# A streaming encoder trunk in fp32: moved weight splits, a delayed recurrence, an earlier attention and a last norm in two halves

## The chip, the cores and the metric

The kernel runs on one core of one Trainium2 chip. The core has a matrix engine (TensorE, PE in the profile; its weight loads are listed apart as PEld), three engines for elementwise work (VectorE = DVE, ScalarE = ACT, GpSimd = POOL), and SyncE (SP), which here issues nearly all transfers between memory and the core. PE writes its sums into banks of the PSUM memory, from which the other engines read. Each engine works through its own list of instructions in order; an instruction that must wait for another engine holds up everything behind it in its list. The metric is the device time of one execution, in microseconds (us).

## The reference

1056 tokens (1024 of a prompt, 32 of a sample with earlier state) pass through two layers of width 1024. Every sublayer ends in a layer norm over the sum with its input.

```python
# layer 0: mLSTM, then SwiGLU; layer 1: attention over a window, then SwiGLU
q, k, v, o, ig, fg = split(x @ w_in)
h = recurrence(q, k * DK**-0.5, v, ig, log_sigmoid(fg), C0, n0, m0)     # 8 heads, chunk by chunk
h = h * rsqrt(mean(h*h) + 1e-6) * g_norm * sigmoid(o)
x = layer_norm(alpha * x + h @ w_out_a)
x = layer_norm(alpha * x + (silu(x @ w_g) * (x @ w_u)) @ w_down)

k, v = split(x @ w_kv)                      # one set, 2 heads of 64; rows of a cache ahead of the sample's
s = (x @ w_q) @ k.T * 64**-0.5 + alibi      # 16 heads; 64-token chunks, own and two before
p = exp(s - max) / (sum(exp(s - max)) + exp(sink - max))
x = layer_norm(alpha * x + (p @ v) @ w_out_b)
x = layer_norm(alpha * x + (silu(x @ w_g) * (x @ w_u)) @ w_down)
```

The outputs are x, the last state of the recurrence, and the keys and values of the last window.

## The kernel before

**Numbers in two halves.** Each fp32 matrix is cut into a high and a low part (`hi` is the value cast to the matrix engine's input type, `lo` is the value less `hi`), and each product is three matmuls: hi·hi, hi·lo, lo·hi (`gemm`, L333 to 344; the three are L341, L342, L343). Activations lie with features across partitions: `ACT` holds the fp32 values and `SX` their parts, 8 tiles of 128 features by 1056 tokens. Tokens are taken in three groups (384, 384, 288), four quarters of 264, or nine chunks of 128 (the last of 32).

**The written order.** The order of all instructions is fixed when the program is built, by a small planner. Dense products are written one k-step (three matmuls) after another; after each step `wv.tick(us)` (class `Weave`, L63) hands the other tasks a time allowance `us` = 3·(max(columns, 256)/2400 + 0.003): 0.339 for 264 columns, 0.329 for 256, 0.489 for 384. A task is a generator that writes some instructions and then yields a pace: the allowance that must pass before it goes on. So a pace is a number of k-steps between two writes, not a time on the chip. `drain` writes the rest of a task at once, with no product between. `pipeline` (L92) runs a chain of stages over items, each stage a given lag behind the one before and with a pace after each step.

**Weights.** Class `Weights` (L119) keeps one list of all weights in order of use. A unit (128 x up to 1024) comes in by a transfer from SP's queue into one of `RAW` = 3 buffers (`wr`), and is split in two halves; or two units together give seven factors, for the FFN tiles that save one product in eight. A split is a cast on ACT (`wh`, L188) and a subtraction (`wl`, L190) on POOL, or on DVE for units listed in `on_vector`. Split halves lie in `SLOTS` = 5 slots, or in a place of their own (`home`). `factor` writes the splits up to the one asked for; `done` frees a unit's slots and writes the next splits as far as slots allow. Since the splits are written at that point, they stand in ACT's and POOL's order behind all that was written before.

**Stages, and where they lie in the span (us).**

- 0 to 93: the input is split, and the q, k, v of the first two heads (a pair) and all gates are projected.
- 93 to 345: the recurrence (`mlstm`, launched by `begin`, L794) is woven between the projections of pairs 1 to 3: three query groups, three key groups, and nine chunks of values (`proj_v`, L534). Its stages are `first`, `pre` (which fetches the rows `nm`, L671, and adds the mask on POOL, L693), `scores` (L703), `values` and `last`. A pair must be finished before the buffers of the pair after next are given out.
- 345 to 440: output gates (`proj_o`, L829), with an exponential on ACT (L836) that empties PE's bank and a chain on DVE after it. The last two feature tiles, 6 and 7, are done group by group while the buffers of the stage are handed over (L880), and after each, two early splits of the output weights are written.
- 440 to 570: output projection A (`mixer_out`, L897), 8 tiles of 8 steps for each of four quarters, with the norm (`ln_task`, L378; `norm_tail`, L442) of a quarter woven under the products of the next: two sums by PE over a 128 x 128 matrix, squares on ACT, products on DVE, at last a scale and shift for each of eight tiles on ACT (L427).
- 570 to 1005: the up projection of the FFN. The first `FIRST` = 2 blocks are plain products (`up_plain`, L1013), while `sums` (L1033) builds sums of the input on the elementwise engines; the others are tiles of seven factors (`up_tile`, L1076), whose results `stage` (L973) sums, splits and sends to memory. A tile's first product is copied out of its bank by ACT (L1094) when the tile has moved on.
- 1005 to 1250: the down projection (L1205); its last part is plain, with the norm (L1265).
- 1250 to 1296: keys and values for each of three groups, and four query tiles of the first group (`k_group`, `v_group`, `q_group`; loop at L1370). `k_part` splits keys into both halves of the partitions (L1308, L1310).
- 1296 to 1484: attention, 72 items (eight pairs of heads by nine chunks). An item's scores (L1424, L1425) go through DVE (a sum and minimum, L1430), ACT (exponential), DVE and POOL (division), PE (transposition), ACT and DVE (split), PE (values) and DVE (`place`). Scores, transposition and values each yield the pace `GAP_A`. The other query projections stand between. Before this, `v_turn` (L1393) turns the values to token-major, and no item's values may be written until all nine chunks are turned.
- 1484 to 1660: output projection B and its norm; 1660 to 2338: the second FFN, the same as the first; 2338 to 2359: the rest of the last norm, after the last product.

In projection B, the weights of the first quarter are read a second time for the other three. Six of eight units of that second reading have places of their own; the first reading uses the five slots. Each tile asks for its halves just before its product (`wcols`, `W.get`).

## Time and profile before

| | before |
| --- | --- |
| median of 3 runs | 2355.39 us (2355.15 to 2357.9) |
| the profiled execution: run / span | 2360.31 / 2358.5 us |
| mean granted TensorE clock | 0.982 |
| PE busy | 2240.9 us, 95% of the span |
| DVE / ACT / POOL busy | 1433.7 / 1025.8 / 1139.2 us |
| moved | 289.72 MB, 123 GB/s |

The profile is of one execution. Its page has the busy time of each engine, the span in 40 slices, the chain of work that ended last, and groups of instructions by line. From the trace come three further views that are used below. *Stretches*: the busy time and number of instructions of each engine between two points of the span, with the granted clock of TensorE, the DMA share and GB/s. *Groups by line and shape*: number, busy time, mean ns of one, then the idle time of the engine directly before them and what ended it. *Timeline*: single instructions as "start, duration, engine, line, operation, output<-inputs, shape"; in square brackets the idle time before it and the instruction that ended that. Times are us from the start of the span. A matmul's duration reaches from its start to its modelled end; the starts of two that follow each other show the rate.

### The profile page before, as it was taken

Reading aid. Unit: us, or ns where it says so; the run is one execution under the profiler, and the core shown is the slowest. Engines: PE = TensorE matmul, PEld = TensorE weight load, DVE = VectorE, ACT = ScalarE, POOL = GpSimd, SP = SyncE. Lnnn points to the kernel's source line nnn. Section 1 sums busy time; section 2 is a strip of 40 time slices with the busy share of each in tenths; the row PEclk is TensorE's granted clock in tenths of the full one; section 3 lists DMA queues with packets and bytes.
Section 4 is the critical chain, followed back from the end, with each engine's and each line's share of the span. In section 5 each row is a group of like instructions: output and inputs, shape, how many; then the busy total and the mean of one; then the engine's idle time right before and its main releaser. Section 6 shows DMA issues by size and latency. Waiting matters only on the chain. (4 is left out here: it accounts for less than half of the span.)

```text
span 2358.5 us, 44346 instructions
## 1 busy us (share of the span) xinstructions
PE 2240.9 (95%) x17218; PEld 2180.1 (92%) x17218; DVE 1433.7 (61%) x2724; ACT 1025.8 (43%) x2306; POOL 1139.2 (48%) x1054
## 2 busy tenths in 40 slices
PE   8899989899999999999999899889999999999997
PEld 8788879899999999999999789789999999999996
DVE  4344456558655555476667678767765555556655
ACT  3343345346444344322246677736434444432124
POOL 1434332326655556554313676724756665654420
PEclk9999999899999999999999999999999999999998
DMA  3111211301333334597423210331244333398712
GB/s 141 61 48 57 54 39 54 135 19 55 146 139 136 146 137 155 182 317 254 162 80 110 70 43 21 102 116 37 82 155 155 146 146 124 131 318 270 243 50 74
DMA packets 165091, 289.72 MB, mean 123 GB/s; under 512 B 15824, under 2 KB 120840, under 8 KB 164880
## 3 DMA queue, kind: packets, MB, share of 16 engines
q1 hardware_dynamic: 160528, 282.56, 35.2%
q10 hardware_dynamic: 4352, 4.33, 0.5%
q8 instruction: 135, 2.21, 0.4%
q14 instruction: 76, 0.62, 0.1%
HBM read 203.89 MB, written 82.94 MB: 122 GB/s over the span
## 5 line engine op out<-in xcount | busy, mean ns | idle before, releaser
L190 POOL TENSOR_TENSOR wl_s<-wr,wh_s 128x512 fp32r<-128x512 f32 x224 | 316.5, 1432 | 316.1 <-ACT wh_s L188 251.5
L341 PE MATMUL d<-sx,wh 128*128 128x264 f32 (+2 forms) x1152 | 374.7, 325 | 19.6 <-ACT sx L371 9.8
L343 PE MATMUL d<-sx,wl 128*128 128x264 f32 (+2 forms) x1152 | 358.7, 311 | 5.1 <-POOL wl L190 5.1
L342 PE MATMUL d<-sx,wh 128*128 128x264 f32 (+2 forms) x1152 | 358.0, 311 | 1.5 <-DVE sx L372 1.5
L188 ACT CAST wh_s<-wr 128x512 fp32r<-128x512 f32 x224 | 136.0, 618 | 328.5 <-DVE wr L167 300.5
L190 POOL TENSOR_TENSOR wl<-wr,wh 128x512 fp32r<-128x512 f32 (+2 forms) x130 | 175.7, 1374 | 208.1 <-ACT wh L188 191.8
L341 PE MATMUL A<-sx,wh_s 128*128 128x264 f32 x896 | 254.6, 284 | 0.0
L342 PE MATMUL A<-sx,wh_s 128*128 128x264 f32 x896 | 254.2, 284 | 0.0
L343 PE MATMUL A<-sx,wl_s 128*128 128x264 f32 x896 | 254.1, 284 | 0.0
L341 PEld LDWEIGHTS d<-sx,wh 128*128 128x128 f32 x1152 | 222.7, 193 | 27.4 <-ACT wh L188 10.8
L343 PEld LDWEIGHTS d<-sx,wl 128*128 128x128 f32 x1152 | 222.1, 193 | 7.5 <-POOL wl L190 7.5
L342 PEld LDWEIGHTS d<-sx,wh 128*128 128x128 f32 x1152 | 223.0, 194 | 2.9 <-DVE sx L372 2.3
L341 PE MATMUL d<-sx,ex 128*128 128x264 f32 x624 | 184.0, 295 | 12.8 <-ACT z L836 6.5
L343 PE MATMUL d<-sx,ex 128*128 128x264 f32 x624 | 181.1, 290 | 6.7 <-DVE ex L190 5.0
L342 PE MATMUL d<-sx,ex 128*128 128x264 f32 x624 | 180.0, 289 | 0.0
L190 POOL TENSOR_TENSOR wl_a<-wr,wh_a 128x512 fp32r<-128x512 f32 x112 | 153.5, 1372 | 41.3 <-ACT wh_a L188 41.3
L343 PEld LDWEIGHTS A<-sx,wl_s 128*128 128x128 f32 x896 | 168.8, 188 | 0.0
L341 PEld LDWEIGHTS A<-sx,wh_s 128*128 128x128 f32 x896 | 168.5, 188 | 0.1
L342 PEld LDWEIGHTS A<-sx,wh_s 128*128 128x128 f32 x896 | 168.4, 188 | 0.0
L1448 POOL TENSOR_SCALAR s<-s,st 128x256 f32<-128x256 f32 (+1 forms) x144 | 122.5, 864 | 58.2 <-DVE st L1446 32.9
L341 PE MATMUL A<-ex,wh_s 128*128 128x264 f32 x448 | 129.1, 288 | 10.9 <-ACT z L1094 10.9
L984 POOL TENSOR_TENSOR z<-z 128x528 fp32r<-128x528 f32 x76 | 111.9, 1472 | 51.4 <-ACT z L983 45.4
(272 smaller groups left out, 7179.8 us busy)
## 6 DMA issues: line engine op xcount, KB each, us to landing
wr<-in_gu SPq DMA_DIRECT2D x96, 512.0 KB, 4.4
hs_x<-z SPq DMA_DIRECT2D x72, 528.0 KB, 3.7
hs_t<-z SPq DMA_DIRECT2D x64, 528.0 KB, 2.9
sx<-hs_x SPq DMA_DIRECT2D x112, 264.0 KB, 5.3
sx<-hs_t SPq DMA_DIRECT2D x64, 264.0 KB, 6.0
ex<-hs_t SPq DMA_DIRECT2D x64, 264.0 KB, 6.0
wr<-in_dn SPq DMA_DIRECT2D x32, 512.0 KB, 6.3
ex<-hs_x SPq DMA_DIRECT2D x32, 264.0 KB, 5.3
```

What stands on the lines that cost most here:

```text
L188: self.nc.scalar.copy(hi, r)
L190: eng.tensor_sub(lo, r, hi.bitcast(F32))
L341: nc.tensor.matmul(out, ah, bh, start=start and k == 0, stop=False, **kw)
L342: nc.tensor.matmul(out, ah, bl, start=False, stop=False, **kw)
L343: nc.tensor.matmul(out, al, bh, start=False, stop=stop and k == last, **kw)
L984: eng.tensor_sub(lo.bitcast(F32R), buf(s), hi)
L1448: nc.gpsimd.tensor_scalar_mul(p[:R, h, lo:256], p[:R, h, lo:256], st[:R, 2, h : h + 1])
```

## The change

1. **Recurrence.** A task `go` with a pace of 5.0 is launched after the recurrence; `pre` may begin only when it has ended. The stage `first` is not held back.
2. **Query weights.** After the second and the fifth chunk of values of pairs 1 to 3 (`c` = 2 and 5), one half of the next unit (query weights of the next pair; after the last, the first output-gate unit) is split, into places of their own. `_next` returns without a split when the place is still held by a unit in use.
3. **Last output gates.** For tiles 6 and 7, `W.done` comes after the two early splits instead of between product and exponential.
4. **Up weights.** The second halves of the plain up units are subtracted on DVE instead of POOL, in both layers (2 blocks x 2 halves of the tokens x 2 units); `sums` yields 2.6 instead of 2.2; `stage` yields 2.0 before its first split.
5. **Attention.** Only the first group's keys, values and queries are made ahead; then all parts of the norm before it and the cached keys and values are written, and the attention is launched. Keys and values of groups 1 and 2 follow, with the attention between. An item's values wait only for their own chunk of `v_turn`. `GAP_A` goes from 0.397 to 0.46. The four output transfers of keys and values come after that.
6. **Output projections** (A and B). Each tile asks for its own halves first, and in the first two quarters has the splits written up to two units ahead.
7. **Last norm.** The last quarter of the last product is done as two groups of 132 columns, with a norm for each; their affine steps of odd tiles are on DVE. Eight tiles of six steps, 144 matmuls of 264 columns, thereby become 288 of 132.

```diff
-GAP_A = 0.397
+GAP_A = 0.46
...
         if key not in self.home and len(self.live) == SLOTS:
+            return False
+        if key in self.home and any(self.home.get(k) is self.home[key] for k in self.parts):
             return False
...
+        on_vector.update((u, 1) for i in range(FIRST) for c in range(2) for u in up[i, c])
...
+    def quarter(g, a=0, n=N4):
+        return slice(g * N4 + a, g * N4 + a + n), (g % 2, slice(a, a + n))
+    QUARTERS = [quarter(g) for g in range(4)]
+    FINAL = [*QUARTERS[:3], quarter(3, 0, N4 // 2), quarter(3, N4 // 2, N4 // 2)]
...
-                    z = ACT[:, k, cols]
-                    nc.scalar.activation(z, z, AF.Identity, scale=lng[:, li, k : k + 1], bias=lnb[:, li, k : k + 1])
+                    z, gk, bk = ACT[:, k, cols], lng[:, li, k : k + 1], lnb[:, li, k : k + 1]
+                    if final and last and k & 1:
+                        nc.vector.tensor_scalar(z, z, gk, bk, op0=ALU.mult, op1=ALU.add)
+                    else:
+                        nc.scalar.activation(z, z, AF.Identity, scale=gk, bias=bk)
...
-        for g in range(4):
+        groups = FINAL if final else QUARTERS
+        for g, (cols, (c, zs)) in enumerate(groups):
...
             mst["v"] += 1
+            if j and c in (2, 5):
+                W.factor((*U_Q, U_O[0])[j + 1], c // 5)
...
-                (pre, lambda j, c: mst["ready"] > j, 1, 0),
+                (pre, lambda j, c: mst["go"] and mst["ready"] > j, 1, 0),
...
         pa2 = ea.enter_context(pool("pa2"))
+        for f in range(2):
+            home = [new(pa2, f"oh{i}", [P, D // 2], F32R, bufs=2)[:] for i in range(2)]
+            W.home.update({(u, f): home for u in [*U_Q[2:], U_O[0]]})
         task = wv.launch(mlstm(GAP_M))
+        wv.launch(go())
+    def go():
+        yield 5.0
+        mst["go"] = True
...
         for m in range(6, 8):
-            proj_o(m, g)
+            proj_o(m, g, False)
             for _ in range(2):
                 W.factor(*early.pop(0))
+            if g == 2:
+                W.done(U_O[m])
...
                 u = us[g > 0][m]
+                W.get(u)
+                if g < 2:
+                    W.split_to(us[g][min(m + 2, KT - 1)])
...
+            yield 2.0
             put("t1", s12, nc.gpsimd, True)
...
-                yield 2.2
+                yield 2.6
...
-    for g in range(3):
-        for t in tasks[: (2, 3, 4)[g]]:
-            wv.drain(t)
-        if g == 1:
-            v_parts(9, cv[:], P)
-            k_part(ck, SEQ, P)
+    def keys_values(g):
         for f, w in ((k_group, U_KV[g > 0][0]), (v_group, U_KV[g > 0][1])):
             f(g)
             if g != 1:
                 W.done(w)
-        if g == 0:
-            for j in range(4):
-                q_group(j, 0)
-                W.done(U_QB[0][j])
+    for t in tasks[:2]:
+        wv.drain(t)
+    keys_values(0)
+    for j in range(4):
+        q_group(j, 0)
+        W.done(U_QB[0][j])
+    for t in tasks[2:]:
+        wv.drain(t)
+    v_parts(9, cv[:], P)
+    k_part(ck, SEQ, P)
...
-                (values, lambda j, b: ast["v"] == 9, 1, gap),
+                (values, lambda j, b: ast["v"] > b, 1, gap),
...
-    wv.launch(v_turn())
+    wv.launch(v_turn(0))
     task = wv.launch(attention((GAP_A,) * 8))
     ast["ready"] = 4
+    for g in range(1, 3):
+        keys_values(g)
+        wv.launch(v_turn(g))
```

79 lines of the change are left out of this document (41 added, 38 removed).

## The prediction

> **What bounds the kernel now.** I read the page first, then the busy times of chosen stretches, then PE's waits in those stretches, then the queue that each wait names. TensorE is the bound: 2240.9 us of the span of 2358.5 us.
>
> ```profile
> PE 2240.9 (95%) x17218; PEld 2180.1 (92%) x17218; DVE 1433.7 (61%) x2724; ACT 1025.8 (43%) x2306; POOL 1139.2 (48%) x1054
> ```
>
> So a change can win only where PE stands still or has a low clock, and loses wherever it gives PE work. The stretches that the change touches (columns: stretch, its length, busy time and count on PE, PEld, DVE, ACT, POOL, then granted clock, DMA share, GB/s):
>
> ```profile
> 93.00:108.00 15.00, 9.70 (x51) 8.21 (x50) 4.73 (x17) 4.19 (x14) 9.15 (x21) 0.77 0.35 102
> 151.00:162.00 11.00, 8.19 (x34) 6.99 (x33) 3.66 (x12) 4.33 (x13) 7.92 (x13) 0.69 0.24 76
> 227.00:231.00 4.00, 2.39 (x14) 1.82 (x13) 1.62 (x8) 2.71 (x7) 2.45 (x2) 1.00 0.00 0
> 302.00:306.00 4.00, 2.38 (x15) 1.73 (x14) 2.66 (x7) 3.34 (x10) 2.31 (x2) 1.00 0.00 0
> 423.00:448.00 25.00, 15.02 (x84) 14.59 (x84) 18.29 (x32) 12.65 (x30) 13.24 (x10) 0.73 0.48 157
> 570.00:578.00 8.00, 6.26 (x37) 5.84 (x36) 7.10 (x7) 4.15 (x8) 6.17 (x6) 0.79 0.22 65
> 1296.00:1318.00 22.00, 15.89 (x74) 13.13 (x73) 9.65 (x41) 11.14 (x38) 11.43 (x16) 0.77 0.29 83
> 1318.00:1476.00 158.00, 149.84 (x1079) 141.43 (x1079) 124.70 (x483) 123.88 (x387) 111.63 (x141) 0.99 0.12 39
> 1476.00:1490.00 14.00, 8.38 (x55) 7.09 (x55) 10.91 (x38) 11.98 (x34) 11.24 (x12) 0.96 0.23 75
> 1535.00:1576.00 41.00, 31.83 (x207) 30.04 (x207) 26.43 (x39) 17.53 (x32) 13.28 (x9) 0.88 0.45 148
> 1662.00:1670.00 8.00, 6.32 (x37) 5.90 (x36) 7.10 (x7) 4.16 (x8) 6.17 (x6) 0.79 0.19 66
> 2318.00:2338.00 20.00, 19.77 (x156) 19.29 (x155) 13.14 (x25) 8.61 (x18) 1.33 (x1) 1.00 0.16 55
> 2338.00:2359.00 21.00, 3.26 (x8) 1.85 (x8) 9.53 (x16) 10.22 (x20) 0.00 (x0) 0.60 0.30 103
> ```
>
> The reader sees stillness (length less PE's busy time) with a granted clock under 1 beside it: after a stop PE gets half its clock for a while. A clock of c over a stretch of L means 2(1-c)L at half speed, which costs at most half of that.
>
> **The change part by part.** Each sum is against this profiled execution (span 2358.5 us, run 2360.31 us); the median of the runs is 2355.39 us, 4.9 us under that run, and I put the difference onto the median.
>
> *Recurrence delayed by 5 us of pace.* PE waits for the first scores:
>
> ```profile
> 100.41 1.19 PE L703 MATMUL S<-qz,kT 128*128 128x256 f32 x2 [4.68 <-DVE p L707]
> 94.85 0.94 SPq L671 DMA_DIRECT2D nm<-scrm  x2
> 98.30 0.72 POOL L693 TENSOR_TENSOR nm<-nm,cmask 128x256 f32<-128x256 f32 x1 [3.79 <-issue]
> ```
>
> Behind the wait lies a fetch issued at 94.85 whose use begins at 98.30. With `go` the fetch lands under projection matmuls. What stays is the chain from there to DVE's product, about 2.1 us (98.30 to 100.41), less a pause of 0.6: some 1.1 us with what overlaps, so 3.6 us go. Half clock, 2x0.23x15 = 6.9 us, cost up to 3.4; I take half, 1.7. What is late next: nine value chunks give 9x8x0.329 = 23.7 us of pace, and pair 0's last placement needs 20.7 of them; 5 more make 25.7, so its last two steps are emitted without projection beside them, 0.8 us. Sum -4.5; bounds -8.1 and +2.
>
> *Query weights split during the values products, in homes of their own.* They remove PE's wait at each new pair:
>
> ```profile
> 154.53 0.69 PE L341 MATMUL d<-sx,wh 128*128 128x384 f32 x1 [2.46 <-ACT wh L188]
> 228.52 0.44 PE L341 MATMUL d<-sx,wh 128*128 128x384 f32 x1 [0.87 <-ACT wh L188]
> ```
>
> Stillness in the three stretches from 151, 227 and 302: 2.8+1.6+1.6 = 6.0 us; half clock in the first 2x0.31x11 = 6.8 us, up to 3.4. No instruction is added: six casts and six subtractions move some 15 us earlier, under proj_v, where the recurrence's POOL steps can take 1.4 us of delay since they run an item ahead. The keys' splits stay behind three query groups. -9; bounds -9.4 and -4.
>
> *Order of the splits around the last output gates.*
>
> ```profile
> 430.30 0.59 PE L341 MATMUL d<-sx,ex 128*128 128x264 f32 x1 [6.46 <-ACT z L836]
> 428.81 1.14 ACT L188 CAST wh<-wr 128x512 fp32r<-128x512 f32 x2 [3.16 <-DMA wr<-in_wout_a]
> 429.85 0.40 ACT L836 ACTIVATE z<-d 128x288 f32<-128x288 f32 x1
> 441.64 0.59 PE L341 MATMUL d<-sx,ex 128*128 128x264 f32 x1 [3.52 <-DVE act L911]
> ```
>
> L836 frees PE's PSUM bank but stands in ACT's order behind casts that wait for a weight transfer. Afterwards the exponential of m=6 stands ahead of them; that of m=7 still stands behind the same transfer, one 2.9 us product later in PE's order. So the first stop shrinks by 2 to 3 us, and the second by less, since DVE's gate chain and POOL's splits keep their length. -3.5; bounds: nothing gained, +1, and all of it with the clock, 10.0+6.7 = -16.7.
>
> *Second halves of the plain up weights split on DVE; sums at a pace of 2.6.* Stillness 1.7+1.7 us (570 and 1662), half clock up to 1.7 each: 6.8 in all. Sixteen subtractions change engine:
>
> ```profile
> L190 DVE TENSOR_TENSOR wl<-wr,wh 128x512 fp32r<-128x512 f32 x10 | 8.0, 832 | 5.1 <-ACT wh L188 5.1
> L190 POOL TENSOR_TENSOR wl<-wr,wh 128x512 fp32r<-128x512 f32 x122 | 166.2, 1386 | 180.5 <-ACT wh L188 164.2 <-PE psS L1425 11.3 <-issue 2.5
> ```
>
> POOL loses 16x1.386 = 22 us, DVE gains 16x0.83 = 13 us where it is already busy 7.1 of 8 us. -3; bounds -6.8 and +3.
>
> *Pause of 2.0 in `stage`.* It looks aimed at this wait, 10.9 us in 16 stops:
>
> ```profile
> L341 PE MATMUL A<-ex,wh_s 128*128 128x264 f32 x448 | 129.1, 288 | 10.9 <-ACT z L1094 10.9
> ```
>
> By the pace, stage begins at the third of the eight steps of the tile's first product, and 2.0/0.339 = 5.9 steps later is the eighth: the cast is still emitted before L1094's copy. ACT's order is the same, so 0; bounds -10.9 and +3.
>
> *Attention begun with the first group's keys, pace 0.46.* Its start now stands still 22-15.9 = 6.1 us and has up to 10 us of half clock, together some 11 us. Afterwards it starts inside the second group's key projection, near 1280, and there DVE is behind:
>
> ```profile
> 1298.61 0.39 PE L1424 MATMUL psS<-KH,Q 128*128 128x256 f32 x1 [2.28 <-DVE st L1430]
> 1281.59 1.04 DVE L1354 TENSOR_TENSOR VR<-cv,VR 128x128 fp32r<-128x128 f32 x1 [0.24 <-ACT VR L1353]
> 1282.55 1.36 DVE L1308 TENSOR_TENSOR KL<-ck,KH 64x128 fp32r<-64x128 f32 x1
> 1283.94 1.20 DVE L1310 CAST KL<-KL 64x128 fp32r<-64x128 f32 x1
> ```
>
> The second scores wait for DVE's L1430 of the first, which is queued behind these rows until about 1286; PE, in order, holds the key projection behind it for some 5.6 us, and loses perhaps 3.5 more to the clock and to the next items. So the start gains 2 rather than 11. In the middle, 158 us hold 8.2 us of stillness; the slower pace may take 2. At the end the pace leaves 57 items placed instead of 59 when the last query group is projected, and 60 are needed before the output projection: two more items with nothing beside them in a stretch that already stands 5.6 of 14 us, +2. Together -2; bounds -14 and +23 (below).
>
> *Output projection B splits two units ahead.*
>
> ```profile
> 1539.16 1.25 PE L395 MATMUL ln<-z,onesm 128*128 128x264 f32 x4 [2.72 <-DVE z L454]
> 1566.94 0.39 PE L341 MATMUL d<-sx,ex 128*128 128x264 f32 x1 [2.85 <-ACT ex L188]
> ```
>
> Of 41-31.8 = 9.2 us of stillness 2.7 is the norm's sum, which no split moves; 6.5 are waits for splits emitted directly before their product. Two products ahead is 5.8 us, against 0.6 (ACT) and 1.4 (POOL). With half clock (2x0.12x41 = 9.8 us) up to 4 more. -8; bounds -10.5 and 0.
>
> *The last norm in two halves.* This gives PE work: 8x6x3 = 144 matmuls of 264 columns become 288 of 132. The quarter now takes 19.8 us for 156 records, 0.127 each. Nearest for 132 columns are the first block's scores, 128 columns with 128 stationary ones:
>
> ```profile
> 1319.97 0.28 PE L1424 MATMUL psS<-KH,Q 128*128 128x128 f32 x1
> 1320.08 0.27 PE L1425 MATMUL psS<-KL,Q 128*128 128x128 f32 x1
> ```
>
> They follow each other at 0.11 us, not at half of 0.127: 288x0.111 = 32.0 against 144x0.122 = 17.5, and 0.5 us for two more small sums, +15. What it saves lies after the last matmul:
>
> ```profile
> 2337.49 0.28 PE L343 MATMUL d<-sx,ex 128*128 128x264 f32 x1
> 2350.98 4.09 ACT L427 ACTIVATE act<-act,lnb,lng 128x264 f32<-128x264 f32 x8 [1.77 <-DVE act L422]
> L422 DVE TENSOR_TENSOR act<-act,z 128x528 f32<-128x528 f32 x64 | 43.9, 731 | 0.6
> L1272 DVE TENSOR_TENSOR act<-act,d 128x264 f32<-128x264 f32 x64 | 27.3, 426 | 42.3 <-PE d L343 42.3
> ```
>
> From 2337.6 to the last activation's end at 2355.1 are 17.5 us; half the width costs 426/731 = 0.6 of it, 10.5; four of eight affines on DVE take 0.8 off, the first half's leftovers put 0.8 on. 7 us are saved, and the 3.4 us behind stay. +8; bounds: -6.5 if matmuls halved, +10.
>
> The Trainium skill, "TensorE: Matmul & The Clock Gate", section "Back-to-back issue gap", gives about 81 ns per matmul at 128 columns in a stream of loads and matmuls. By it the 288 would take 23.3 us and this part come to 0 instead of +8. The row above says 0.11 us, and I go by the row.
>
> Sum: -4.5-9-3.5-3+0-2-8+8 = -22 us: 2336.5 of span, 2333 us for the median.
>
> **The rivals.**
> - *All aimed-at waits go.* The start of the attention saves 9, the recurrence 8, the gates 9, the up weights 6, the middle 3, with -9 and -9 for the two that I count nearly whole, and +8 at the end: -45, 2310 us. For it: each wait has its part. Against: DVE's rows at 1281 and the transfer at 428.81.
> - *PE pays for the attention inside the key projections: slower.* The early start puts 12 items among 14 us of key and value matmuls. If each costs PE 1.6 us of stop, as the first stops at 1298 cost 2.3, that is 19, with 5.6 at its beginning 25 where I count 9 and save 11: the part turns from -2 to +14, and with half clock over the same stretch, 8 us more, to +22. Decides from about 1.6 us an item: 2355 and above; with that clock and the end's two items at 4 us each, 2359. Against: the middle stretch shows 8.2 us of stillness in 158.
> - *The splits only trade places.* ACT and POOL keep order, so an early split delays another step: only the query splits (-9) and the tail (+8) show, 2354 us.
> - *The 81 ns rate.* As a mechanism: loads overlap better in a long run than in the four matmuls shown; 0.081 each makes 23.3 us of the 32.0, 2325 us. For it speaks only that the sample is short.
>
> **How the numbers follow.** My forecast has 0.48 (its own range 2320 to 2346), all waits gone 0.20, slower attention 0.15, traded places 0.12, faster tail 0.05. The measurement can tell about 0.2%, 4.7 us: faster is below 2350.7. Traded places straddle it (0.04 faster, 0.05 same, 0.03 slower): faster 0.77, same 0.05, slower 0.18. The range 2309 to 2356 leaves out the upper part of the slower case and a little below.
>
> **What would show it.** The waits at L703, at L341 for wh near 152, 227 and 302, and at L341 and L343 for ex near 1549 to 1568 should be gone; L1094's sixteen stops should stay; PE should wait once some 5 us for L1430 inside the second keys; the last quarter should take about 34 us and the stretch after it 14. The prediction is wrong if key projections and attention stop each other item by item, or if 132-column matmuls run well under 0.11 us.

## The result, and the profile after

| | before | changed |
| --- | --- | --- |
| median | 2355.76 us (2350.62 to 2361.97) | 2361.42 us (2357.66 to 2365.57) |
| ratio to before | | 1.0024, interval 1.0017 to 1.0031 |
| profiled execution: run / span | 2360.31 / 2358.5 us | 2360.58 / 2357.5 us |
| mean granted clock | 0.982 | 0.985 |

The changed kernel is 5.7 us slower; the forecast was 22 us faster. The two profiles alone would mislead: the one of before is 4.6 us over its kernel's median, so their spans differ by only 1.0 us the other way. In the profile of the changed kernel the line numbers are shifted: the three matmuls of a product are L344, L345, L346 (before: L341 to L343), a split's cast and subtraction L190 and L192 (L188, L190), the gates' exponential L864 (L836), the reduction of scores L1462 (L1430).

The page's busy line of the changed kernel:

```profile
PE 2246.9 (95%) x17370; PEld 2190.0 (93%) x17370; DVE 1459.9 (62%) x2772; ACT 1026.3 (44%) x2313; POOL 1114.8 (47%) x1038
```

Stretches of the changed kernel that answer to those of before (stretch, length, busy time and count on PE, PEld, DVE, ACT, POOL, granted clock, DMA share, GB/s):

```profile
93.00:108.00 15.00, 14.78 (x118) 13.63 (x116) 3.75 (x14) 3.86 (x14) 9.00 (x19) 1.00 0.36 102
148.00:158.00 10.00, 6.05 (x32) 5.42 (x31) 4.38 (x13) 5.30 (x19) 7.74 (x13) 0.85 0.47 144
418.00:443.00 25.00, 16.33 (x94) 15.84 (x93) 21.33 (x33) 13.08 (x31) 14.62 (x10) 0.73 0.51 166
548.00:578.00 30.00, 26.77 (x210) 25.62 (x209) 23.48 (x27) 19.83 (x39) 16.80 (x12) 1.00 0.22 70
1272.00:1296.00 24.00, 16.65 (x95) 15.23 (x95) 17.82 (x54) 16.43 (x50) 14.67 (x19) 0.79 0.29 88
1318.00:1472.00 154.00, 146.32 (x1039) 137.27 (x1038) 114.35 (x433) 114.15 (x354) 102.52 (x126) 1.00 0.13 40
1530.00:1571.00 41.00, 37.97 (x287) 37.05 (x287) 31.54 (x49) 21.63 (x40) 13.34 (x11) 0.96 0.49 167
2308.60:2343.50 34.90, 34.90 (x306) 34.55 (x304) 19.52 (x48) 13.83 (x30) 1.32 (x1) 1.00 0.18 63
2343.50:2357.50 14.00, 1.99 (x9) 1.46 (x8) 7.94 (x25) 5.75 (x14) 0.00 (x0) 0.60 0.27 78
```

The first row shows PE without a stop where it stood 5.3 us of 15 before; the second shows 4 us of stillness in a place of the same stage; the row from 1530 shows 3 us of stillness where there were 9.2; the last quarter now takes 34.9 us and the rest 14.0.

Because single profiles of one kernel scatter, I measured each stage between the same two instructions in the profiles of all kernels below and took means of those with a part of the change and those without. Profiles of kernels that carry only a piece of a stage's part are left out of its row. All lengths are in us; in brackets stand the shortest and the longest single profile. The forecast's -3 for the up weights is shared out to the two layers.

| stage, from and to | without the part | with it | difference | forecast |
| --- | --- | --- | --- | --- |
| recurrence: last value copy of pair 0 to the ninth exponential of the gates | 295.5 (295.1 to 296.9) | 292.8 (290.0 to 296.7) | -2.7 | -13.5 |
| last gates: 19th exponential to the sixth tile of projection A | 49.3 (48.8 to 50.1) | 48.8 (48.1 to 49.3) | -0.5 | -3.5 |
| FFN of layer 0: end of projection A to end of the last down product | 714.7 (712.7 to 716.4) | 716.9 (715.0 to 719.6) | +2.2 | -1.5 |
| keys and attention: from there to the first parts for projection B | 234.8 (232.7 to 236.0) | 237.6 (236.4 to 238.5) | +2.8 | -2 |
| projection B: from there to its last tile | 139.8 (139.3 to 140.8) | 130.8 (129.3 to 131.9) | -9.0 | -8 |
| FFN of layer 1: from there to the third quarter of the last product | 692.1 (691.3 to 692.9) | 695.8 (694.2 to 697.2) | +3.7 | -1.5 |
| last norm: from there to the end of the span | 39.8 (39.5 to 40.4) | 48.3 (48.2 to 48.8) | +8.5 | +8 |

The differences sum to +5.0 us, the medians differ by 5.7. So nothing large lies outside these stages. (The rest of projection A, which part 6 of the change also touches, takes 83.9 us in the kernel before and 84.0 in the changed one.) (The third row holds a wait for the first down weights that scatters by some 3 us.)

### The profile page after: what moved, and what is told of

It reads as the page before. It is cut to its first block, busy times and chain, and to the rows that moved or that the text cites. A ratio compares the mean times of both kernels' runs of the same rounds, so it can differ in the third digit from the quotient of the medians.

```text
span 2357.5 us, 44628 instructions
## 1 busy us (share of the span) xinstructions
PE 2246.9 (95%) x17370; PEld 2190.0 (93%) x17370; DVE 1459.9 (62%) x2772; ACT 1026.3 (44%) x2313; POOL 1114.8 (47%) x1038
## 5 line engine op out<-in xcount | busy, mean ns | idle before, releaser
L192 POOL TENSOR_TENSOR wl_s<-wr,wh_s 128x512 fp32r<-128x512 f32 x224 | 315.2, 1427 | 303.0 <-ACT wh_s L190 230.7
L344 PE MATMUL d<-sx,wh 128*128 128x264 f32 (+3 forms) x1092 | 350.0, 321 | 12.8 <-ACT sx L374 8.7
L346 PE MATMUL d<-sx,wl 128*128 128x264 f32 (+3 forms) x1092 | 335.4, 307 | 7.6 <-POOL wl L192 7.6
L345 PE MATMUL d<-sx,wh 128*128 128x264 f32 (+3 forms) x1092 | 334.6, 306 | 0.7 <-DVE sx L375 0.7
L190 ACT CAST wh_s<-wr 128x512 fp32r<-128x512 f32 x224 | 135.5, 617 | 332.3 <-DVE wr L167 300.7
L344 PE MATMUL A<-sx,wh_s 128*128 128x264 f32 x896 | 254.9, 284 | 2.8 <-ACT z L1143 2.8
L345 PE MATMUL A<-sx,wh_s 128*128 128x264 f32 x896 | 254.2, 284 | 0.0
L346 PE MATMUL A<-sx,wl_s 128*128 128x264 f32 x896 | 254.0, 283 | 0.0
L192 POOL TENSOR_TENSOR wl<-wr,wh 128x512 fp32r<-128x512 f32 (+2 forms) x108 | 143.2, 1345 | 183.4 <-ACT wh L190 178.5
L344 PEld LDWEIGHTS d<-sx,wh 128*128 128x128 f32 x1092 | 208.6, 191 | 18.5 <-ACT sx L374 9.4
L346 PEld LDWEIGHTS d<-sx,wl 128*128 128x128 f32 x1092 | 207.9, 190 | 10.2 <-POOL wl L192 10.2
L345 PEld LDWEIGHTS d<-sx,wh 128*128 128x128 f32 x1092 | 208.6, 191 | 2.4 <-DVE sx L375 1.6
L344 PE MATMUL d<-sx,ex 128*128 128x264 f32 (+1 forms) x660 | 192.5, 292 | 8.7 <-DVE act L944 5.0
L346 PE MATMUL d<-sx,ex 128*128 128x264 f32 (+1 forms) x660 | 189.1, 286 | 3.3 <-DVE ex L192 3.3
L345 PE MATMUL d<-sx,ex 128*128 128x264 f32 (+1 forms) x660 | 188.8, 286 | 0.0
L192 POOL TENSOR_TENSOR wl_a<-wr,wh_a 128x512 fp32r<-128x512 f32 x112 | 156.5, 1405 | 47.4 <-ACT wh_a L190 47.4
L344 PEld LDWEIGHTS A<-sx,wh_s 128*128 128x128 f32 x896 | 168.4, 188 | 3.6 <-ACT z L1143 3.6
L346 PEld LDWEIGHTS A<-sx,wl_s 128*128 128x128 f32 x896 | 168.9, 188 | 0.0
L345 PEld LDWEIGHTS A<-sx,wh_s 128*128 128x128 f32 x896 | 168.4, 188 | 0.0
L1480 POOL TENSOR_SCALAR s<-s,st 128x256 f32<-128x256 f32 (+1 forms) x144 | 122.5, 863 | 63.0 <-DVE st L1478 39.8
L1017 POOL TENSOR_TENSOR z<-z 128x528 fp32r<-128x528 f32 x76 | 111.2, 1463 | 67.7 <-ACT z L1016 67.4
L344 PE MATMUL A<-ex,wh_s 128*128 128x264 f32 x448 | 129.7, 289 | 9.4 <-ACT z L1128 9.4
```

The source lines that it names most:

```text
L190: self.nc.scalar.copy(hi, r)
L192: eng.tensor_sub(lo, r, hi.bitcast(F32))
L344: nc.tensor.matmul(out, ah, bh, start=start and k == 0, stop=False, **kw)
L345: nc.tensor.matmul(out, ah, bl, start=False, stop=False, **kw)
L346: nc.tensor.matmul(out, al, bh, start=False, stop=stop and k == last, **kw)
L1017: eng.tensor_sub(lo.bitcast(F32R), buf(s), hi)
```

## The experiments

A, B and C are the cases that the text on record ahead of each run sets out.

### The kernel before, once more

Edit: none. 

> The kernel before, unchanged, for a second profile. The two profiles at hand differ by only 1.0 us of span (2358.5 and 2357.5), while the medians differ by 5.7 us (2355.76 and 2361.42). Theory A: the first profile of before was a slow sample, about 4.5 us over its median; this one's span lies near 2353, and the 4.5 us are found in one or two stretches with more stops or a lower clock. Rival B: profiles of this kernel always come out some 4 us above its median, and the span is again near 2358. The ratio of times is 1.000 within 0.001.

Measured: 2358.22 us, ratio 1.0009 (1.0000 to 1.0018), span 2356.4. Between A and B: a profile's span lies about 2 us below its run's time, and this sample too is over its kernel's median. The 2.1 us to the first profile are not one wait: they come and go over several stages (-1.2 at the last gates, -2.1 in the attention, +1.4 in projection B). What follows: differences of 2 us between two single profiles prove nothing, hence the table above.

### Last norm in quarters

```diff
-    FINAL = [*QUARTERS[:3], quarter(3, 0, N4 // 2), quarter(3, N4 // 2, N4 // 2)]
+    FINAL = QUARTERS
...
-                    if final and last and k & 1:
+                    if False:
```

> The changed kernel with the last norm in four quarters again (no groups of 132 columns, affines on ACT). Theory A, the forecast's step: 288 matmuls at 0.111 us cost 15 us, the shorter tail gives back 7; without it the kernel is 8 to 9 us faster than the changed one, 2352 to 2353, ratio to before 0.998 to 0.999. Rival B: tail and matmuls balance, or the end is set by the output transfers: 2361, ratio 1.0024. Rival C: the halves gain: slower than 2364.

Measured: 2354.83 us, ratio 0.9994 (0.9986 to 1.0003). The stage measures 39.5 us against 48.2 in the changed kernel. The changed kernel's matmuls of 132 columns in the timeline (start, duration):

```profile
2342.61 0.28 PE L346 MATMUL d<-sx,ex 128*128 128x132 f32 x1
2342.72 0.27 PE L344 MATMUL d<-sx,ex 128*128 128x132 f32 x1
2342.83 0.28 PE L345 MATMUL d<-sx,ex 128*128 128x132 f32 x1
```

They start 0.11 us apart, as the four short score matmuls of the forecast did; 264 columns took 0.12. Half as wide costs nearly as much each. The stage's 8.7 us are A's 8 to 9. The time, 6.6 us under the changed kernel, is a little short of A, but far from B and C.

### Attention as before

```diff
-GAP_A = 0.46
+GAP_A = 0.397
...
-    keys_values(0)
+    for g in range(3):
+        for t in tasks[: (2, 3, 4)[g]]:
+            wv.drain(t)
...
-                (values, lambda j, b: ast["v"] > b, 1, gap),
+                (values, lambda j, b: ast["v"] == 9, 1, gap),
```

> The changed kernel with the attention as before: all keys first, values after all nine turns, pace 0.397. Theory A, from the two profiles: from the first keys to the parts of the first group the changed kernel loses 1.5 us against the one before (from 5.2 ahead to 3.7 ahead); so this one is 1 to 2 us faster than the changed kernel, about 2360. Rival B, the forecast's -2: the early start gains, this one takes 2363 to 2364. Rival C, the forecast's slower case: the early start costs 14 us or more, this one takes 2347 or less. The stop of 5.1 us of PE for the first reduction of scores (near 1275) goes, and stops of 2.3 and 1.7 us near 1296 and 1314 come back.

Measured: 2360.30 us, ratio 1.0022 (1.0013 to 1.0032): 1.1 us under the changed kernel, by itself within the scatter; the attention's stage measures 235.8 instead of 237.5. C is excluded, A and B are not told apart by the time alone; the attention alone, below, does that. The stop that the forecast named is there in the changed kernel (timeline of DVE and PE):

```profile
1276.44 1.00 DVE L1388 TENSOR_TENSOR VR<-cv,VR 128x128 fp32r<-128x128 f32 x1 [0.24 <-ACT VR L1387]
1277.36 1.34 DVE L1342 TENSOR_TENSOR KL<-ck,KH 64x128 fp32r<-64x128 f32 x1
1278.74 1.17 DVE L1344 CAST KL<-KL 64x128 fp32r<-64x128 f32 x1
1280.72 0.28 DVE L1462 CUSTOM_DVE_ANT_0 s<-psS,bt 128x129 f32<-128x129 f32 x1
1281.07 0.58 PE L1456 MATMUL psS<-KH,Q 128*128 128x256 f32 x1 [5.11 <-DVE st L1462]
```

PE waits 5.1 us for a reduction of 0.28 us that stands behind the parts of the cached values and keys.

### Recurrence not delayed, query weights not split early

```diff
-                (pre, lambda j, c: mst["go"] and mst["ready"] > j, 1, 0),
+                (pre, lambda j, c: mst["ready"] > j, 1, 0),
...
-            if j and c in (2, 5):
-                W.factor((*U_Q, U_O[0])[j + 1], c // 5)
```

> The changed kernel without the delay of the recurrence and without the early splits of the query weights. Theory A, from the two profiles: those parts gave 5.2 us (0.7 behind at 93, 4.5 ahead at the output gates), so this one takes about 2366 to 2367. Rival B, the forecast's sum: 13.5 us, 2375. Rival C: the recurrence's own chain sets the end of this stage, and what the projections gain is waited away: 2361 to 2362.

Measured: 2363.73 us, ratio 1.0036 (1.0022 to 1.0050): 2.3 us over the changed kernel, between A and C; the stage measures 295.2, as in the kernel before. The forecast's 13.5 are excluded. Where they went is seen in the changed kernel at the change of pairs (timeline, ordered by engine):

```profile
148.31 2.17 ACT L190 CAST wh<-wr 128x512 fp32r<-128x512 f32 x4
148.99 4.96 POOL L192 TENSOR_TENSOR wl<-wr,wh 128x512 fp32r<-128x512 f32 x4 [1.31 <-ACT wh L190]
140.15 0.30 DVE L776 TENSOR_TENSOR small<-small 128x2 f32<-128x2 f32 x1 [0.39 <-ACT small L772]
140.49 0.19 DVE L777 TENSOR_TENSOR small<-small 128x2 f32<-128x2 f32 x1
151.35 0.18 DVE L773 TENSOR_SCALAR small<-small 128x2 f32<-128x2 f32 x1 [3.87 <-ACT junk L766]
151.92 0.83 DVE L776 TENSOR_TENSOR small<-small 128x2 f32<-128x2 f32 x1 [0.38 <-ACT small L772]
152.78 1.19 DVE L777 TENSOR_TENSOR small<-small 128x2 f32<-128x2 f32 x1
155.08 0.70 PE L742 MATMUL T<-vt,ks 128*64 128x129 f32 x4 [3.95 <-DVE act L790]
```

When the last values are done, `W.done` still writes four splits at once (the query weights were there already, so the four are the next ones). Their casts stand on ACT before the squares of a recurrence item (L766), DVE waits 3.9 us for those, and two of its smallest operations take 0.83 and 1.19 us instead of 0.30 and 0.19 while POOL subtracts. PE, whose next instruction belongs to the recurrence, stands 4.0 us. Before, it stood 2.5 us at the same time for the query split itself. The wait was exchanged.

The exchange shows in the whole stage. From the last value copy of pair 0 to the first gate exponential, PE's idle time ahead of projections is 10.3 us in the mean of the six profiles without these parts and 2.3 in the seven with them; ahead of the recurrence's own instructions it is 5.8 and 11.8 us. The last value copy of pair 3 comes 7.9 us earlier (298.0 instead of 305.8), but the last item of the recurrence is placed no earlier (356.3 instead of 355.7).

### Key splits spread over the query groups

```diff
-        W.done(ua)
-        W.done(ub)
+        W.done(ua, fill=j == 0)
+        W.done(ub, fill=j == 0)
...
                 proj_q(j, g)
+                if j > 1 and g < 2:
+                    W.factor(U_K[j], g)
...
             proj_o(m, g, g == 2)
+            if m == 0 and g < 2:
+                W.factor(U_O[1], g)
```

With `fill=False`, `done` only frees the slots and writes no splits.

> The changed kernel, but the last chunk of a pair's values no longer writes four weight splits at once: the two halves of the next key weights are written after the first and the second query group (for the output gates: of the second gate unit after the first two products). Theory A: the waits for the query splits were only exchanged for a wait behind those four splits: four casts on ACT (2.16 us) and four subtractions on POOL (4.95 us) stand before the recurrence's squares, and PE stops 4.5, 3.0 and 0.8 us near 152, 235 and 306 for the copy that places the item before. Those stops go, and with the clock the kernel gains 5 to 8 us: 2353 to 2356. Rival B: the recurrence's own chain of items sets the end of the stage: the stops go, but as much is waited at the first output gates, between 313 and 360; the time stays at 2360 to 2362.

Measured: 2356.20 us, ratio 0.9999 (0.9990 to 1.0008), 5.2 us under the changed kernel. The group in which PE waits for the copy that places an item, in the changed kernel and then in this one (count, busy time, mean ns, idle time before and what ended it):

```profile
L742 PE MATMUL T<-vt,ks 128*64 128x129 f32 x128 | 14.4, 303 | 9.0 <-DVE act L790 8.7
```

```profile
L742 PE MATMUL T<-vt,ks 128*64 128x129 f32 x128 | 14.1, 299 | 6.4 <-DVE act L790 6.4
```

The stops at the changes of pairs fall to 1.3 us and less; 3.45 us of the 6.4 that are left lie at 317, in the recurrence's end. The mechanism of A is right, and B holds for a part: at the first gate exponential this profile is 10.0 us ahead of the changed kernel's, at the ninth 4.0. From the first to the ninth the kernel before takes 46.6 us (mean of six), the changed one 50.7 (of seven), this one 56.4. Part of this is work that now falls there: 84 of PE's instructions in that stretch belong to the recurrence in the kernel before, 98 in the changed one, 101 here. Part is waiting: all of PE's idle time there, 5.2, 7.1 and 8.3 us, is ahead of the recurrence's instructions. The 36 items follow each other, and what the projections gain is partly waited for there. Still, the whole stage is 6.0 us shorter than the mean of the changed kernel's: so much of the miss is due to the four splits.

### Splits spread, no delay

Edit: the one above, and the delay taken out as in the kernel with the old recurrence.

> The kernel with the spread key splits, and the recurrence not delayed by the pace of 5. Theory A: the recurrence's chain of items sets the end of the stage (with spread splits the projections were 18.0 us ahead at the first output gate, and 8.5 at the ninth); starting it earlier brings its end forward by 3 to 5 us although PE stops some 4.8 us for the first scores near 95: 2351 to 2353. Rival B: the stop and its half clock cost as much as the start gains: 2356 to 2357. Rival C: the projections set the end after all, and the delay's 3.6 us are lost: 2360.

Measured: 2361.78 us, ratio 1.0024 (1.0016 to 1.0033): C, 5.6 us slower than with the delay. The stage measures 293.0 against 286.8. The first scores again stop PE:

```profile
L721 PE MATMUL S<-qz,kT 128*128 128x256 f32 x64 | 19.7, 389 | 5.4 <-DVE p L725 4.8 <-POOL qz L704 0.6
```

So with spread splits the delay is worth 5.6 us, near the 4.5 that the forecast gave it. A, by which the recurrence's chain alone sets the end and an earlier start brings that end forward, is excluded: the last item is placed at 352.3 us here and at 350.4 with the delay.

### The delay alone

Edit: the kernel before with `go()` and its condition in `pre`, nothing else.

> The kernel before with the recurrence delayed by the pace of 5 and nothing else changed. Theory A, the forecast's term: -4.5, 2351 to 2352; the stop of 4.7 us near 95 shrinks to 1.5 or less, the stops for the query splits near 152, 228 and 303 stay. Rival B: what is won at the start is waited at the end of the recurrence: 2356. Rival C: the items come later and the stage ends later: 2358 to 2361.

Measured: 2359.58 us, ratio 1.0014 (1.0004 to 1.0023): slower, C. The stop for the first scores shrinks to 1.5 us, as forecast, and at pair 2's first query group the profile is 4.4 us ahead of the one of before; at the ninth gate exponential it is 4.3 us behind. Part of the loss is here (timeline of PE):

```profile
227.42 0.69 PE L343 MATMUL d<-sx,wh 128*128 128x384 f32 x1 [5.60 <-ACT wh L190]
```

The wait for pair 3's query split was 0.87 us before; it is 5.6 with the delay. This profile's first fetch was one of the late ones (last section), so its size may not be typical; the time of all its runs says slower all the same. The three edits of this stage are not a sum (the early splits alone were not run): delay alone +4 (time), early splits and delay -2.7, early and spread splits without delay about -2.5, all three together -8.3 (287.2, mean of three profiles, against 295.5).

### Up halves on POOL again

```diff
-        on_vector.update((u, 1) for i in range(FIRST) for c in range(2) for u in up[i, c])
```

> The changed kernel with the second halves of the plain up weights subtracted on POOL again (the pace of the sums stays 2.6). Theory A: on DVE these subtractions stand before the last quarter's norm and delay its affines and, behind them in ACT's order, the casts of weights, by 1.75 us; PE stops four times per layer for a subtraction (0.84, 0.54, 0.88, 0.78). With them on POOL there are two such stops per layer or fewer, and the kernel gains 1 to 1.5 us per layer: 2358 to 2359.5. Rival B: the pace of the sums makes the stops: nothing changes, 2361. Rival C, the forecast's step: DVE relieves POOL, so this one is slower by 3 us: 2364.

Measured: 2359.84 us, ratio 1.0015 (1.0006 to 1.0024), 1.6 us under the changed kernel. In the changed kernel PE stops once per two products for a subtraction on POOL. On DVE a product of the norm (L433) stands behind the moved subtraction, which waits 2.5 us for its cast; the next affines and casts on ACT come after that product (timeline of ACT, DVE and PE):

```profile
553.05 1.14 ACT L190 CAST wh<-wr 128x512 fp32r<-128x512 f32 x2
554.22 1.34 DVE L192 TENSOR_TENSOR wl<-wr,wh 128x512 fp32r<-128x512 f32 x1 [2.50 <-ACT wh L190]
555.49 0.70 DVE L433 TENSOR_TENSOR act<-act,z 128x528 f32<-128x528 f32 x1
555.07 0.39 PE L346 MATMUL d<-sx,wl 128*128 128x264 f32 x1 [0.84 <-POOL wl L192]
568.84 0.39 PE L346 MATMUL d<-sx,wl 128*128 128x264 f32 x1 [0.88 <-POOL wl L192]
```

With the halves on POOL the FFN of layer 1 measures 692.7 us against a mean of 695.8 with them on DVE and 692.1 without the whole part: by this profile 3.1 of 3.7 us come from this list of weights, 0.6 from the paces. The 3.1 may be too much: PE's idle time in the stage falls by 1.0 only. The rest is PE's busy time, with a granted clock of 1.0000 in the stage here and of 0.9975 in the changed kernel. The profile of "Cached parts written earlier", with the halves on DVE and a clock of 1.0000, measures 694.2, which leaves 1.5. In layer 0 the up tiles take 471.8 against 473.4 and 470.7. The four stops per layer for POOL's subtraction (3.0 us) become two (1.3), as A has it, but a new stop of 1.4 us for a cast near 567 takes back most of that. The time is too coarse to confirm 3 us.

### The last gates without splits between

```diff
-            for _ in range(2):
+            for _ in range(2 if g < 2 else 0):
                 W.factor(*early.pop(0))
             if g == 2:
-                W.done(U_O[m])
+                W.done(U_O[m], fill=False)
```

> The changed kernel, but in the last token group the products of the gate tiles 6 and 7 come first, without weight splits between or before their exponentials (four early splits are left to the output projection, which writes them two units ahead). Theory A: the second stop (5.0 us, for the reduction that frees the bank before the output projection) is ACT's exponential of tile 7 behind casts that wait for a transfer; without those it shrinks by 2 to 3 us, and the first by as much or less: 2357 to 2359. Rival B: the chain on DVE and the splits of the gated tiles set the stop: 2361, with the stop at 5 us.

Measured: median 2355.85 us, ratio 1.0007 (0.9996 to 1.0017). The stage measures 45.7 us against 48.8. The stops in the changed kernel, and then here:

```profile
425.94 0.59 PE L344 MATMUL d<-sx,ex 128*128 128x264 f32 x1 [3.66 <-ACT z L864]
436.57 0.59 PE L344 MATMUL d<-sx,ex 128*128 128x264 f32 x1 [5.01 <-DVE act L944]
```

```profile
423.62 0.39 PE L344 MATMUL d<-sx,ex 128*128 128x264 f32 x1 [0.55 <-ACT z L864]
430.51 0.59 PE L344 MATMUL d<-sx,ex 128*128 128x264 f32 x1 [3.70 <-ACT ex L190]
433.53 0.59 PE L346 MATMUL d<-sx,ex 128*128 128x264 f32 x1 [2.20 <-POOL ex L192]
```

The first stop goes, the second becomes the wait for the splits themselves. 3 us are gained of the 8.7 of stops; A. The median lies 5.6 us under the changed kernel's, more than A and more than the stage accounts for.

### The old pace with the early start

```diff
-GAP_A = 0.46
+GAP_A = 0.397
```

> The changed kernel with the attention's pace of 0.397 again, its early start kept. Theory A, the forecast's terms: the slower pace gains some 2 us in the middle and gives 2 back at the end, where fewer items are placed: 2360 to 2362. Rival B: the slower pace costs more at the end than it gains: 2357 to 2359. Rival C: without it the items written among the second and third keys come closer and stop PE more often: 2364 or more. The stop of 5.1 us at 1275 stays in all three.

Measured: 2379.28 us, ratio 1.0101 (1.0087 to 1.0114): C, 17.9 us over the changed kernel. The stage measures 262.2 us instead of 237.6, of which projection B gives back 7.6. The scores' group of the changed kernel, then of this one:

```profile
L1456 PE MATMUL psS<-KH,Q 128*128 128x256 f32 x112 | 32.3, 307 | 11.3 <-DVE st L1462 8.2 <-DVE Q L1369 2.6 <-ACT t L1524 0.2
```

```profile
L1456 PE MATMUL psS<-KH,Q 128*128 128x256 f32 x112 | 34.1, 319 | 15.2 <-DVE Q L1369 7.9 <-DVE st L1462 5.4 <-DVE Q L1372 0.9
```

Items now wait for the split of their own queries (L1369): started early, at this pace they have caught up with the query projections, which in turn may be only a few groups ahead of the items. Over all shapes of these scores the waits for L1369 grow from 2.6 to 11.3 us; the rest of the loss was not traced to one wait. The slower pace is not an extra; the early start needs it.

### The pace alone

Edit: `GAP_A = 0.46` in the kernel before.

> The kernel before with the attention's pace at 0.46 and nothing else changed. Theory A, the forecast's terms: 2 us gained in the middle, 2 us given back at the end: 2355 to 2357. Rival B: items now fall behind the query projections, and what is left runs with nothing beside it before the output projection: 2360 to 2370. Rival C: the pace was too close for the engines and the gain in the middle is larger: 2350 to 2353.

Measured: 2357.22 us, ratio 1.0008 (0.9999 to 1.0018): A, not distinguishable from no change; the stage measures 235.8, without it 234.8. The waits change their kind (transpositions, kernel before and then this one):

```profile
L1468 PE MATMUL T<-ident,s 128*128 128x128 f32 x240 | 40.4, 283 | 9.5 <-POOL s L1448 3.3 <-DVE lo L1472 3.1 <-DVE st L1446 2.3
```

```profile
L1468 PE MATMUL T<-ident,s 128*128 128x128 f32 x240 | 39.6, 285 | 19.0 <-DVE lo L1472 15.0 <-DVE st L1446 2.6 <-POOL s L1448 0.9
```

### The attention alone

Edit: the kernel before with part 5 of the change, nothing else.

> The kernel before with the attention's part of the change alone (first group's keys, values by chunk, pace 0.46). Theory A, from the profiles of nine kernels: between the last down product and the parts of the first group the early start costs about 3 us: 2358 to 2360. Rival B, the forecast's -2: 2353 to 2355. Rival C, the forecast's slower case of +14: 2368 or more.

Measured: 2359.26 us, ratio 1.0017 (1.0008 to 1.0027), that is +1.9 to +6.4 us. A: the early start costs some 3 us, the sign of the forecast's -2 is wrong, and its slower case of +14 is wrong too.

### Cached parts written earlier

```diff
     for t in tasks[2:]:
         wv.drain(t)
-    v_parts(9, cv[:], P)
-    k_part(ck, SEQ, P)
...
     keys_values(0)
+    v_parts(9, cv[:], P)
+    k_part(ck, SEQ, P)
```

> The changed kernel with the parts of the cached keys and values written right after the first group's values instead of just ahead of the attention. Theory A, the forecast's mechanism: the 5.1 us stop near 1275 is DVE's five rows for the cached parts (1276.4 to 1280.5, 4.1 us) ahead of the first reduction; without them it shrinks to about 1 us, and with the clock 4 to 7 us are gained: 2354 to 2357. Rival B: the queries' splits, now behind those rows, stop the second query product instead, or the second item waits for its chain through the engines: 2359 to 2361.

Measured: 2357.98 us, ratio 1.0017 (1.0005 to 1.0029). PE's stops near the start of the attention:

```profile
1273.84 0.52 PE L344 MATMUL d<-sx,wh 128*128 128x384 f32 x1 [3.55 <-ACT wh L190]
1277.91 0.58 PE L1456 MATMUL psS<-KH,Q 128*128 128x256 f32 x1 [1.07 <-DVE st L1462]
```

The stop of 5.1 us falls to 1.1, as A has it; the wait for the last query weights ahead of it grows from 1.8 to 3.6. The stage measures 235.1 instead of 237.6. Between A and B.

### Splits two units ahead, alone

Edit: the kernel before with part 6 of the change, nothing else.

> The kernel before with one part of the change alone: in the output projections each tile asks for its own halves first, and in the first two quarters splits are written up to two units ahead. Theory A, the forecast's term: -8 (the profiles with the change showed 8.7 to 9.7 us between the parts of the first group and the end of projection B): 2346 to 2348, ratio 0.996 to 0.997; the stops of 2.85, 1.15 and 0.8 us for splits near 1548 to 1568 are gone. Rival B: in the kernel before, the splits ahead delay the attention's last items on ACT and POOL: 2352 to 2356.

Measured: 2344.25 us, ratio 0.9959 (0.9944 to 0.9974): A, a little beyond it. All that stops PE for over 0.25 us between 1520 and 1575 are the norm's sums; a third such stop is of 0.5 us:

```profile
1532.81 1.13 PE L405 MATMUL ln<-z,onesm 128*128 128x264 f32 x4 [2.20 <-DVE z L468]
1546.53 1.16 PE L419 MATMUL ln<-z,onesm 128*128 128x264 f32 x4 [1.68 <-DVE z L414]
```

### What holds, combined

Edit: the changed kernel with the quarters, the old attention, the up halves on POOL, sums at 2.2 and no pause in `stage`, and with the spread key splits and the mended gates.

> The changed kernel with what the runs spoke against undone or mended: last norm in quarters, attention as before, up halves on POOL, sums at 2.2, no pause in the stage; key splits spread over the query groups; the last gates without splits between. What stays of the change: the early query splits, the delay of the recurrence, the splits two units ahead. Theory A: the single gains add (6.6 for the quarters, 5.2 for the spread, 5.6 for the gates, 1.1 for the attention, 1.6 for the up halves, together 20): 2341 to 2344, ratio 0.994 to 0.995. Rival B: some of them are the same microseconds, or noise of the single runs: 2346 to 2350.

Measured: 2333.61 us, ratio 0.9910 (0.9894 to 0.9925): the fastest kernel of the study, 22 us under before and 27.8 under the changed one. That is faster than both expectations, and more than the 20 of the single gains; the most that was undercounted is in the FFN stages, which are 4.2 and 2.9 us shorter than the changed kernel's means, where 1.6 was counted for both. Its page's busy line; its span is 2331.8 us:

```profile
PE 2226.2 (95%) x17218; PEld 2168.7 (93%) x17218; DVE 1441.0 (62%) x2724; ACT 1024.8 (44%) x2306; POOL 1142.0 (49%) x1054
```

Against the means without the parts, recurrence 286.2, gates 45.7 and projection B 131.6 give -9.3, -3.6 and -8.2, together -21.1 us.

### The combination with the early attention

Edit: that kernel with part 5 of the change and the cached parts written earlier.

> The combined kernel with the changed attention (early start, pace 0.46) and the cached parts written after the first group's values. Theory A: the early start costs 3 us and the cached parts give 2.7 back: 2333 to 2335, no difference from the combined kernel (2333.6). Rival B: with that stop gone the early start wins: 2326 to 2331. Rival C: it still costs: 2337 to 2340.

Measured: 2337.09 us, ratio 0.9916 (0.9902 to 0.9929). The median lies in C, but the intervals overlap with those of the combined kernel, so that A and C are not told apart; B, a gain, is excluded. Even mended, the early start wins nothing.

## Why the prediction was wrong

The forecast was 2333 us in a range of 2309 to 2356; the time is 2361.4. By its steps:

- *Recurrence delayed, -4.5, bounds -8.1 and +2: failed.* The step named the first wait rightly; it is gone. But it priced this wait by PE's stillness and took for granted that the end of the stage follows; of the recurrence's own end it looked at pair 0's last placement, not at pair 3's. With both parts of this stage the last item is placed no earlier than before. Alone the delay costs 4 us, a value outside the bounds, and only with splits that do not hold the recurrence is it worth -5.6. Why it costs alone is not shown; in its one profile the last item is placed at 363.2 us, and a wait of 5.6 us stands ahead of that.
- *Query weights, -9, bounds -9.4 and -4: failed, the largest miss.* "Six casts and six subtractions move" was complete for the query weights; what the step left out is that `done` fills the freed slots with four other splits at the old place. The waits for `wh` near 152, 227 and 303 are gone as foretold, and PE waits there for the recurrence, behind those four. This and the step above: -2.7 where -13.5 was summed. Spreading the four gives 6.0 of the missing 10.8 us; how the other 4.8 divide between the recurrence's chain and the gates stays open.
- *Order around the last gates, -3.5: mis-sized.* The first stop fell from 6.5 to 3.7 us, as said; the second grew from 3.5 to 5.0, where "by less" was expected. -0.5.
- *Up halves on DVE, -3, bounds -6.8 and +3: wrong sign.* The step showed DVE busy for 7.1 of 8 us and still took a gain. The subtractions delay the last quarter's norm on DVE, its affines on ACT, and the casts behind them. The FFN stages cost +2.2 and +3.7; of the latter 1.5 to 3.1 are due to these halves. The first is clouded by the wait for down weights.
- *Pause in `stage`, 0: right for the wait that it named, but not free.* The waits for ACT's copy of the tile, now L1128, keep their place: 9.4 us against 10.9. But PE now also waits for another copy out of the same bank (L1143), in three stops, where the kernel before has none; that copy itself waits 0.8 to 0.9 us each time for a subtraction of `stage` (L1017). No run separates the pause from the pace of the sums here. The group in the changed kernel:

```profile
L344 PE MATMUL A<-sx,wh_s 128*128 128x264 f32 x896 | 254.9, 284 | 2.8 <-ACT z L1143 2.8
```

- *Attention, -2, bounds -14 and +23: wrong sign, small.* The wait of 5.6 us for L1430, drawn from three DVE rows, came at 5.1 us. The missing part is the pace: costed at +2 and -2, it holds the early start up; without it the change would cost another 18 us.
- *Projection B, -8: right*, -9.0 in the table, -9.7 by the ratio of the part alone (0.9959 of 2356).
- *Last norm, +8: right*, +8.5; the quarter takes 34.9 us and the rest 14.0, where 34 and 14 were named. The estimate of 0.111 us for 132 columns, taken from four score matmuls, is within 1% of the 0.112 us between the starts of these 288. The Trainium skill, "TensorE: Matmul & The Clock Gate", section "Back-to-back issue gap", gives about 81 ns for 128 columns. These matmuls measure 112 ns, so the rival built on the 81 fell, and the measurement decides.

Of the rivals, "the splits only trade places" (2354) had the right idea, that an early split delays another step, but at the wrong place: it kept the -9 of the query weights, where just this happened, and denied the gain in projection B, which came. "Attention slower" named the nearest times (2355 to 2359), but by a part that costs 2.8 us, not 14; and its sum does not close, since +14 in place of -2 makes 2349 and +22 makes 2357. The forecast's error of 27 us is 10.8 in the recurrence, 8.9 in the two FFN stages, 4.8 in the attention and 3.0 at the gates, less 0.5 for the two steps that were right.

## What to carry to other kernels

Before a wait of the busiest engine is priced, ask which chain of dependent items ends the stage; if it is another chain, the removed wait comes back at that chain's end or inside it. When a piece of work is written earlier, look at what the planner then writes at the old place: a freed slot is filled at once, and those instructions stand in front of somebody. An edit that loses alone can gain beside another: the delay cost 4 us alone and gained 5.6 with the splits spread.

## What the runs showed of the hardware that I had not expected

- Matmuls of 132 columns start 0.11 us apart, those of 264 columns 0.12: in this stream, each with its own weight load, half the width saves under a tenth.
- Two DVE operations on 128x2 elements (L776, L777) take 0.83 and 1.19 us while POOL's 1.24 us subtractions run, against 0.30 and 0.19 without them, and 0.15 to 0.16 for the 28 and 30 of 36 in the changed kernel's profile that meet no POOL instruction. L773, which reads one tensor, keeps 0.18 beside the same subtractions. The Trainium skill, "SBUF — State Buffer", section "Terms", describes a port pair that the two engines share and that one of them locks for a whole instruction; these rows agree with that.
- From the issue of the recurrence's first fetch to POOL's first use of it pass 3.4 to 3.9 us in 14 of the 18 profiles and 5.2 to 5.6 in four; all of the late ones are of kernels with the delay. Of the seven profiles behind the value 292.8 in the table's first row, the three with the late fetch measure 295.9, 296.7 and 291.4, the four others 290.0 to 293.4. What makes the fetch late, and whether it alone makes the scatter, stays open.
